# A hybrid DeltaNet and neighbourhood-attention layer on one core: PSUM pools that wait by bank, one more empty step before a group of transposes, and another order of the first loads

## The chip, the cores and the metric

The kernel runs on one core of one Trainium2 chip. The core has a matmul engine (TensorE, PE in the rows), a vector engine (VectorE, DVE), a scalar engine (ScalarE, ACT), a general one (GpSimd, POOL), and a synchronisation engine (SyncE, SP) that here only issues DMAs. Each engine runs its own instructions in order, and waits on semaphores for the others. SBUF is the on-chip memory that all of them read. PSUM is the memory that matmuls write, in eight banks of 128 x 512 fp32.

The metric is the device time of one execution in microseconds (us), the median of several runs.

## The reference

One layer, on 1024 latent tokens and 256 context tokens, of width 1024:

```python
mod_x = silu(c) @ w_ada + b_ada                    # shift, scale, gate, twice; the same for the context
px = modulate(rms_norm(x, norm1_w), sh1, sc1) @ w_in
pc = modulate(rms_norm(ctx, norm1_w), csh1, csc1) @ w_in
dn_c, s_f, s_b = gated_deltanet(pc[..., :DN_IN], ..., zeros, zeros)   # 4 heads of 128, chunks of 64
dn_x, _, _ = gated_deltanet(px[..., :DN_IN], ..., s_f, s_b)           # both directions
na_x = neighborhood_attention(qx, kx, vx, kc, vc, na_rpb, rows)       # 8 heads of 64, 8 x 16 window
x = x + g1 * (concat([dn_x, na_x]) @ w_out)
x = x + g2 * swiglu(modulate(rms_norm(x, norm2_w), sh2, sc2), w_ffn_in, w_ffn_out)
```

The DeltaNet group needs, for each chunk, the inverse of a unit lower triangular matrix I + M, where M is made of the keys' products kk, the decays g and the betas.

## The kernel before

Matrix products are done on fp32 values that are split into a rounded part and a remainder: three matmuls for each product, hi x hi, hi x lo and lo x hi. Normed and modulated tokens lie in `hh` and `hl` (eight tiles of 128 features x 1280 tokens, 256 of them context), weights in `whi` and `wlo`. `whi` is made by a cast (L201 or, on ScalarE, L203) of a raw tile `wraw` (or `fraw`, for the first two blocks), and `wlo` by a subtraction (L204, on POOL but for the first block, where DVE does it).

The first part of the program, up to the attention, is a list of jobs. A job is one column block of the input projection: eight k-steps of nine matmuls L413 into three banks `blk` (256, 512 and 512 tokens), or a `Wide` job, with tokens on the partitions, by L609. The order is k0, k1 (these two together, in the opening part, L757 and L413), k2, k3, z (second half), nk0, nk1, nk2, nv, nk3, q0 to q3, nq0 to nq3, v0, nv, v1 to v3, z (first half). Between the k-steps the code of the loop advances other work one step at a time, by Python generators: the `finish` of an earlier block (transposes L537, the products kk L561 and their copies L562), its `norm` (L502 to L516), and a background list `bg` that holds `block_inverses` and then `preps`. A `yield` without work in such a generator is an empty step: the work after it is issued one k-step later, and so stands further down in the order of every engine that takes part.

`block_inverses` begins with `decay_tables` (small DVE operations that give G, then L842 on TensorE), builds the matrices in `WK` (L865, L878, L880), transposes them on TensorE in four groups of eight (L900, `m<-cst,WK`), each group in two banks that ScalarE copies to `N` (L902). Then it inverts by back substitution on DVE (L910 and L912, for c from 30 down to 1, one c each k-step), and transposes back (L922).

In the opening part ScalarE squares the token tiles `xt`, TensorE sums them (L742), and the first modulation follows: `ada(j)` multiplies the 1 MB weight tile `wada` j with silu(c) (L706), the result is copied to `arow` (L708), `column(j)` brings it to the partitions (L714, L716, L719), and `normed_tile(k)` makes hh and hl (L726 and L729 on DVE, L727 on ScalarE). SP issues the loads on one queue, in the order of the code.

PSUM is handed out by pools, one after another. The opening part and k2, k3, z use `psb`, the jobs from nk0 on `psa` (four `blk` banks, two `m`, two `pr`), the last job and the attention `psg` (two tiles `sc` of three banks, two banks `ps`), and the output projection and the rest `psf` (eight banks). A new pool opens where an old one is closed. With no option given, every tile of the new pool waits for every user of the released ones.

## Time and profile before

| | us |
|---|---|
| median of 3 runs | 1517.0 (1516.87 to 1519.63) |
| the profiled execution | 1512.36 |
| its span | 1510.6 |
| TensorE busy in it | 1462.2 (97%) |
| VectorE, ScalarE, GpSimd busy | 996.8, 703.5, 236.7 |
| granted TensorE clock, mean | 0.996 of full |

Rows of the profile begin with the start (us from the span's start), the time that the merged group took, engine, line and operation; `out<-in` are the program's tile names; in brackets at the end stands the idle time of the engine just before, and what ended it. Rows of waits name the waiting and the releasing instruction, then the total in us, the count and the longest. A line number is that of the kernel before; in the changed kernel lines stand 7 to 13 further down.

### The profile page before, as it was taken

How to read it: one execution, taken by the hardware profiler on the slowest of the kernel's cores; microseconds unless marked ns; L12 is line 12 of the kernel's file. 1: busy time of each engine (PE TensorE's matmuls, PEld its weight loads, DVE VectorE, ACT ScalarE, POOL GpSimd, SP SyncE). 2: the span in 40 equal slices, each digit the busy share in tenths (PEclk: the TensorE clock that was granted, in tenths of full speed). 3: DMA queues.
4: the chain of work that ended last, by engine and by line, in shares of the span. 5: the costliest groups of instructions: out<-in, count | busy, mean ns of one | idle time of the engine just before them, and what ended most of it. 6: DMA issues, size and time to landing. Idle time of an engine off the chain costs nothing.

```text
span 1510.6 us, 23890 instructions
## 1 busy us (share of the span) xinstructions
PE 1462.2 (97%) x8702; PEld 1223.5 (81%) x8702; DVE 996.8 (66%) x1716; ACT 703.5 (47%) x1389; POOL 236.7 (16%) x286
## 2 busy tenths in 40 slices
PE   6999999999999998999999999999999999999998
PEld 3788797877788877887878888888888888888887
DVE  5773589875463745778867389766665567598652
ACT  5453442456663246656853284333333334354440
POOL 1054601456652201111210000000000000000000
PEclk9999999999999999999999999999999999999999
DMA  9274122778665569998539205433333335798742
GB/s 389 75 215 143 54 78 72 244 222 248 195 191 174 157 187 291 290 263 279 163 112 343 79 28 166 141 105 105 105 105 105 105 105 174 260 360 279 251 140 84
DMA packets 205398, 267.36 MB, mean 177 GB/s; under 512 B 15968, under 2 KB 113760, under 8 KB 204256
## 3 DMA queue, kind: packets, MB, share of 16 engines
q1 hardware_dynamic: 197680, 260.01, 53.2%
q10 hardware_dynamic: 7600, 5.81, 1.2%
q8 instruction: 69, 1.13, 0.3%
q14 instruction: 49, 0.40, 0.1%
HBM read 201.02 MB, written 68.94 MB: 179 GB/s over the span
## 4 chain that ended last, share of the span: by engine, by line
PE 51%; ACT 1%; DVE 1%; issue 0%; DMA 0%; POOL 0%; DVEq 0%; POOLq 0%; ACTq 0%
PE ps L1398 28%; PE ps L1741 14%; PE ps L1527 3%; PE ps L1375 1%; PE ps L1549 1%; PE sc L332 1%; PE sc L322 1%; PE sc L309 1%; PE ps L1252 0%; PE ps L1261 0%; DMA z<-z_d 0%; ACT sq L1302 0%; ACT bt L315 0%; DVE bt L313 0%; PE ps L223 0%
## 5 line engine op out<-in xcount | busy, mean ns | idle before, releaser
L1459 ACT CAST uhi<-wq 128x512 fp32r<-128x512 f32 x101 | 61.3, 622 | 135.9 <-issue 84.6
L413 PE MATMUL blk<-hh,whi 128*128 128x512 f32 (+1 forms) x410 | 121.0, 389 | 1.6 <-ACT kk L562 1.4
L1459 ACT CAST uhi<-ws 128x512 fp32r<-128x512 f32 x91 | 54.0, 621 | 146.3 <-PE ps L1398 91.4
L413 PE MATMUL blk<-hl,whi 128*128 128x512 f32 (+1 forms) x410 | 113.4, 370 | 0.3 <-DVE hl L729 0.3
L609 PE MATMUL blk<-zw,hh 128*128 128x256 f32 (+1 forms) x576 | 112.3, 289 | 1.0 <-ACT cr L461 1.0
L413 PE MATMUL blk<-hh,wlo 128*128 128x512 f32 (+1 forms) x410 | 112.0, 370 | 0.6 <-POOL wlo L204 0.6
L1460 DVE TENSOR_TENSOR ulo<-wq,uhi 128x512 fp32r<-128x512 f32 x101 | 67.6, 688 | 59.1 <-ACT uhi L1459 32.7
L1398 PE MATMUL ps<-hT,uhi 128*128 128x512 f32 x336 | 103.7, 390 | 0.0
L1398 PE MATMUL ps<-lT,uhi 128*128 128x512 f32 x336 | 103.4, 389 | 0.0
L1398 PE MATMUL ps<-hT,ulo 128*128 128x512 f32 x336 | 103.4, 389 | 0.0
L609 PEld LDWEIGHTS blk<-zw,hh 128*128 128x128 f32 x576 | 90.7, 189 | 4.1 <-ACT cr L461 1.4
L1398 PE MATMUL ps<-hB,uhi 128*128 128x512 f32 x288 | 89.1, 390 | 0.0
L1398 PE MATMUL ps<-lB,uhi 128*128 128x512 f32 x288 | 88.7, 389 | 0.0
L1398 PE MATMUL ps<-hB,ulo 128*128 128x512 f32 x288 | 88.7, 389 | 0.0
L413 PEld LDWEIGHTS blk<-hh,wlo 128*128 128x128 f32 x410 | 71.0, 188 | 14.8 <-POOL wlo L204 0.9
L413 PEld LDWEIGHTS blk<-hl,whi 128*128 128x128 f32 x410 | 71.2, 188 | 14.4 <-DVE hl L729 0.8
L609 PE MATMUL blk<-zw,hl 128*128 128x256 f32 (+1 forms) x288 | 81.9, 284 | 0.0
L413 PEld LDWEIGHTS blk<-hh,whi 128*128 128x128 f32 x410 | 67.6, 190 | 16.8 <-issue 3.8
L204 POOL TENSOR_TENSOR wlo<-wraw,whi 128x1024 fp32r<-128x1024 f32 x18 | 44.8, 2488 | 186.8 <-ACT whi L203 186.5
L1398 PEld LDWEIGHTS ps<-lT,uhi 128*128 128x128 f32 x336 | 63.1, 188 | 13.1
L1398 PEld LDWEIGHTS ps<-hT,ulo 128*128 128x128 f32 x336 | 63.1, 188 | 13.1
L1398 PEld LDWEIGHTS ps<-hT,uhi 128*128 128x128 f32 x336 | 62.9, 188 | 13.0
(361 smaller groups left out, 3500.7 us busy)
## 6 DMA issues: line engine op xcount, KB each, us to landing
wq<-w_fo SPq DMA_DIRECT2D x99, 256.0 KB, 4.2
wq<-w_gu SPq DMA_DIRECT2D x88, 256.0 KB, 2.9
wad<-wa SPq DMA_DIRECT2D x64, 256.0 KB, 4.3
bt<-rpb SPq DMA_DIRECT2D x64, 192.0 KB, 3.9
t_d<-g SPq DMA_DIRECT2D x22, 512.0 KB, 3.5
fr<-t_d SPq DMA_DIRECT2D x44, 256.0 KB, 4.9
f_d<-g SPq DMA_DIRECT2D x33, 256.0 KB, 2.1
fr<-f_d SPq DMA_DIRECT2D x33, 256.0 KB, 4.2
```

Of the source, the lines that this page charges most:

```text
L204: lo_engine.tensor_tensor(o, r, h.bitcast(F32), OP.subtract)
L309: s = pe.matmul(sc[:, u * 640 + n0:u * 640 + n1], q, ks[i], start=i == 0, stop=i == 1)
L322: pe.transpose(sc[:, u * 640 + j * 128:u * 640 + (j + 1) * 128], bt[:, j * 128:(j + 1) * 128], ident)
L332: pe.matmul(sc[u * ND:u * ND + ND, 1280:1408], vv, pt[:, j * 128:(j + 1) * 128], start=j == 0, stop=j == 4)
L413: pe.matmul(o, ww[:, k], xx[k][:, s], start=k == 0 and j == 0, stop=k == KT - 1 and j == 2)
L609: pe.matmul(p[:, :c1 - c0], x[k][:, s], ww[:, k, c0:c1], start=k == 0 and j == 0, stop=k == KT - 1 and j == 2)
L1375: pe.matmul(o, w[wi][:, k], parts[xi][k][:, s], start=k == 4 and j == 0, stop=k == 3 and j == 2)
L1398: pe.matmul(o, w[wi][:, k], x[xi][:, k], start=first and k == 0 and j == 0, stop=k == n - 1 and j == 2, skip_group_check=True)
L1459: act.copy(hi, self.raw[key])
L1460: dve.tensor_tensor(lo, self.raw[key], hi.bitcast(F32), OP.subtract)
L1527: pe.matmul(o, w[wi][:, k], parts[xi][k][:, s], start=k == 0 and j == 0, stop=k == KT - 1 and j == 2)
L1741: pe.matmul(o[b], w[wi][:, b], F[xn, p][xi], start=n in (0, 1, 5) and p == 0 and j == 0, stop=p == NFB // 2 - 1 and j == 2, skip_group_che ...
```

## The change

Three things are changed.

1. The pools `psa`, `psg` and `psf` are opened so that a tile waits only for the users of earlier tiles in its own bank. For the last job the two `sc` tiles get a pool of their own, `psc`, which is opened ahead of `psg` and of which the first tile is taken at once, so that `sc` lies in the first six banks and `ps` in the last two.
2. In `block_inverses` there are five empty steps and not four ahead of the first transposes L900, and none behind the last step of the back substitution: the transposes stand one k-step later, the rest of the work where it was.
3. `wada` 0 is loaded ahead of the two `fraw`; `ada(0)` is written ahead of the two weight splits; and the subtraction that makes the first block's `wlo` (DVE) is put off, into `normed_tile(0)`, between its three L726 and its three L729.

```diff
@@ -62,6 +62,13 @@
     live = [g for g in gens if g is not None]
     while live:
         live = [g for g in live if next(g, 0) != 0]
+
+
+class Deferred:
+
+
+    def tensor_tensor(self, *args):
+        self.args = args
 
 
 class Background:
@@ -292,7 +299,7 @@
         def pair(heads, bts, vw, vc, half, cb, out):
 
             r0 = 4 * half
-            sc = psum[-1].tile([128, 1536], F32, name="sc", tag="sc", bufs=2)
+            sc = psc.pop() if len(psc) > 1 else psc[0].tile([128, 1536], F32, name="sc", tag="sc", bufs=2)
             mx = nw.tile([128, 2, 4], F32, name="mx", tag="mx", bufs=3)
             for u, (head, w0, bt) in enumerate(zip(heads, WIN, bts)):
                 qs, kh, kl = head
@@ -368,7 +375,7 @@
         next(old)
         store(*done)
 
-    na, kept = [], []
+    na, kept, psc = [], [], []
 
     def store(out, hp, half):
 
@@ -680,9 +687,10 @@
                 sp.dma_start(x, a["xcT"][k])
                 xt.append(x)
             raws = [xp.tile([128, KT, 128], F32, name=f"fraw{i}", tag=f"fraw{i}") for i in range(2)]
+            load_ada(0)
             for i in range(2):
                 sp.dma_start(raws[i], a["w_conv"][4 + i])
-            for j in range(3):
+            for j in range(1, 3):
                 load_ada(j)
             sp.dma_start(cst, a["cst"])
             sp.dma_start(masks, a["masks"])
@@ -718,13 +726,15 @@
                                       [128, 2, 2]), OP.add)
                 dve.tensor_scalar(w1s[:, j], m[:, 1], 1.0, n1w[:, j:j + 1], op0=OP.add, op1=OP.mult)
 
-            def normed_tile(k, cuts=(slice(0, CT), slice(CT, T))):
+            def normed_tile(k, cuts=(slice(0, CT), slice(CT, T)), between=None):
                 t = xt[k]
                 parts = [(x, mod1[:, k, int(x.start < CT):int(x.start < CT) + 1]) for x in cuts]
                 for x, sh in parts:
                     j = int(x.start < CT)
                     dve.scalar_tensor_tensor(t[:, x], t[:, x], w1s[:, k, j:j + 1], rs[:, x], op0=OP.mult, op1=OP.mult)
                     act.activation(hh[k][:, x], t[:, x], AF.Identity, bias=sh)
+                if between:
+                    dve.tensor_tensor(*between.args)
                 for x, sh in parts:
                     dve.scalar_tensor_tensor(hl[k][:, x], t[:, x], sh, hh[k][:, x].bitcast(F32),
                                              op0=OP.add, op1=OP.subtract)
@@ -743,11 +753,12 @@
                 for p, s in zip(sums, segs):
                     act.activation(rs[:, s], p[:, :s.stop - s.start], AF.Ln, bias=b_eps, scale=1.0 / D)
                 act.activation(rs, rs, AF.Exp, scale=-0.5)
-                first[0].prefetch(raws[0], dve, dve)
+                ada(0, dve.tensor_copy)
+                kept_lo = Deferred()
+                first[0].prefetch(raws[0], kept_lo, dve)
                 first[1].prefetch(raws[1], pool, pool)
-                ada(0, dve.tensor_copy)
                 column(0)
-                normed_tile(0, segs)
+                normed_tile(0, segs, kept_lo)
                 ada(1, act.copy)
                 for b in first:
                     b.banks()
@@ -890,10 +901,8 @@
                         if not d:
                             yield
                     dve.transpose(fl(KKc), fl(Wc[1]))
-                    yield
-                    yield
-                    yield
-                    yield
+                    for _ in range(5):
+                        yield
                     for i0 in range(0, 32, 4):
                         p = bank()
                         for i in range(4):
@@ -910,7 +919,8 @@
                     dve.tensor_tensor(t, N[:P, :, 0:c, c:c + 1].to_broadcast([P, 4, c, w]),
                                       N[:P, :, c:c + 1, c + 1:32].to_broadcast([P, 4, c, w]), OP.mult)
                     dve.tensor_tensor(N[:P, :, 0:c, c + 1:32], N[:P, :, 0:c, c + 1:32], t, OP.add)
-                    yield
+                    if c != 30:
+                        yield
                 flat = N.rearrange("p b r c -> p b (r c)")
                 dve.memset(flat[:P, :, 0:1024:33], 1.0)
                 for _ in range(7):
@@ -1090,7 +1100,7 @@
             j = jobs[n] if n < len(jobs) else None
             if n == inv:
                 early.close()
-                psum.append(psa.enter_context(tc.tile_pool(name="psa", bufs=1, space=PSUM)))
+                psum.append(psa.enter_context(tc.tile_pool(name="psa", bufs=1, space=PSUM, reuse_waits="tile")))
                 bg.add(block_inverses())
                 bg.add(preps())
             final = n == len(jobs) - 1
@@ -1102,7 +1112,9 @@
                 next(fill)
             if final:
                 psa.close()
-                psum.append(scan_psum.enter_context(tc.tile_pool(name="psg", bufs=1, space=PSUM)))
+                psc.append(scan_psum.enter_context(tc.tile_pool(name="psc", bufs=1, space=PSUM, reuse_waits="tile")))
+                psc.append(psc[0].tile([128, 1536], F32, name="sc", tag="sc", bufs=2))
+                psum.append(scan_psum.enter_context(tc.tile_pool(name="psg", bufs=1, space=PSUM, reuse_waits="tile")))
             if n + 1 < len(jobs):
                 jobs[n + 1].prefetch()
             fin = blk(n - 2) if n - 2 not in done else None
@@ -1357,7 +1369,7 @@
         store(out, 3, half)
     attn.close()
     load_w = weights(wp)
-    ps = ctx.enter_context(tc.tile_pool(name="psf", bufs=8, space=PSUM))
+    ps = ctx.enter_context(tc.tile_pool(name="psf", bufs=8, space=PSUM, reuse_waits="tile"))
 
     def bank(name="ps"):
         return ps.tile([128, 512], F32, name=name, tag="ps")
```

Three places show what moves. The loads on SP at the start, before:

```order
L680 DMA xt_156<-xcT 128x1280
L680 DMA xt_158<-xcT 128x1280
L684 DMA fraw_160<-w_conv 128x1024
L684 DMA fraw_161<-w_conv 128x1024
L676 DMA wada<-wa 128x2048 x3
```

and after:

```order
L687 DMA xt_156<-xcT 128x1280
L687 DMA xt_158<-xcT 128x1280
L683 DMA wada<-wa 128x2048
L692 DMA fraw_160<-w_conv 128x1024
L692 DMA fraw_161<-w_conv 128x1024
L683 DMA wada<-wa 128x2048 x2
```

The first of the eight `wada` has passed both `fraw`. DVE there, before:

```order
L740 TENSOR_TENSOR sq_220<-sq_219,sq_220 128x512 x2
L201 CAST whi<-fraw_160 128x1024
L204 TENSOR_TENSOR wlo<-fraw_160,whi 128x1024
L708 COPY arow<-pm 128x256
L716 TENSOR_TENSOR mod_99<-pm,prm 128x2x2
L719 TENSOR_SCALAR w1s<-mod_99,prm 128x2
L726 SCALAR_TENSOR_TENSOR xt_144<-xt_144,w1s,rs 128x256
L726 SCALAR_TENSOR_TENSOR xt_144<-xt_144,w1s,rs 128x512 x2
L729 SCALAR_TENSOR_TENSOR hl_130<-xt_144,mod_99,hh_129 128x256
```

and after:

```order
L750 TENSOR_TENSOR sq_220<-sq_219,sq_220 128x512 x2
L716 COPY arow<-pm 128x256
L208 CAST whi<-fraw_160 128x1024
L724 TENSOR_TENSOR mod_99<-pm,prm 128x2x2
L727 TENSOR_SCALAR w1s<-mod_99,prm 128x2
L734 SCALAR_TENSOR_TENSOR xt_144<-xt_144,w1s,rs 128x256
L734 SCALAR_TENSOR_TENSOR xt_144<-xt_144,w1s,rs 128x512 x2
L737 TENSOR_TENSOR wlo<-fraw_160,whi 128x1024
L739 SCALAR_TENSOR_TENSOR hl_130<-xt_144,mod_99,hh_129 128x256
```

The copy of `arow` now stands ahead of the cast, and the subtraction behind the three products with `xt`. POOL's order does not change: it splits the second `fraw`, and then the weights of the later blocks.

The third place is job nk2. ScalarE there, before (N<-m are the copies L902, hl the norm's cast L515 of an earlier block, whi the cast of the next weights, cacc<-blk the emptying of nk2's own banks L446):

```order
L503 ACTIVATE cr<-m,bias 128x512
L503 ACTIVATE cr<-pr,bias 128x512
L203 CAST whi<-wraw 128x1024
L507 ACTIVATE cr<-cr 128x1280
L515 CAST hl_1623<-cacc 128x1280
L902 COPY N<-m 80x128x4 x8
L203 CAST whi<-wraw 128x1024
L446 ACTIVATE cacc<-blk 128x256
L446 ACTIVATE cacc<-blk 128x512 x2
```

and after:

```order
L514 ACTIVATE cr<-cr 128x1280
L522 CAST hl_1623<-cacc 128x1280
L911 COPY N<-m 80x128x4 x6
L210 CAST whi<-wraw 128x1024
L453 ACTIVATE cacc<-blk 128x256
L911 COPY N<-m 80x128x4 x2
L453 ACTIVATE cacc<-blk 128x512 x2
```

The last two copies to N now stand behind the cast and behind the first emptying. On TensorE the end of that job reads, before (L900 are the transposes, hh_458 belongs to the last k-step):

```order
L413 MATMUL blk<-hh_456,wlo 128x256
L413 MATMUL blk<-hh_456,wlo 128x512 x2
L900 MATMUL m<-cst,WK 80x128 x8
L413 MATMUL blk<-hh_458,whi 128x256
L413 MATMUL blk<-hh_458,whi 128x512 x2
L413 MATMUL blk<-hl_459,whi 128x256
L413 MATMUL blk<-hl_459,whi 128x512 x2
L413 MATMUL blk<-hh_458,wlo 128x256
L413 MATMUL blk<-hh_458,wlo 128x512 x2
L502 MATMUL m<-cr,cst 128x256
L502 MATMUL m<-cr,cst 128x512
L502 MATMUL pr<-cr,cst 128x512
```

and after:

```order
L420 MATMUL blk<-hh_458,wlo 128x256
L420 MATMUL blk<-hh_458,wlo 128x512 x2
L909 MATMUL m<-cst,WK 80x128 x8
L509 MATMUL pr<-cr,cst 128x512
L509 MATMUL m<-cr,cst 128x256
L509 MATMUL m<-cr,cst 128x512
```

Each group has moved down by one k-step, the last one to right ahead of the norm's matmuls.

## The prediction

> **What bounds the kernel now.** I read the page first (span, busy times, the chain that ended last), then the list of what TensorE waited for, then the clock by windows, and last the order of time around each place that the edits touch.
>
> The page of the kernel before:
>
> ```profile
> span 1510.6 us, 23890 instructions
> ...
> PE 1462.2 (97%) x8702; PEld 1223.5 (81%) x8702; DVE 996.8 (66%) x1716; ACT 703.5 (47%) x1389; POOL 236.7 (16%) x286
> ...
> PE ps L1398 28%; PE ps L1741 14%; PE ps L1527 3%; PE ps L1375 1%; PE ps L1549 1%; PE sc L332 1%; PE sc L322 1%; PE sc L309 1%; PE ps L1252 0%; PE ps L1261 0%; DMA z<-z_d 0%; ACT sq L1302 0%; ACT bt L315 0%; DVE bt L313 0%; PE ps L223 0%
> ```
>
> TensorE is busy for 1462.2 of 1510.6 us, so only 48.4 us can be won without removing matmuls, and the change removes none. The last row is the chain that ended last: nearly half of the span, the stretch from L1375 to the end, hangs on TensorE's own matmuls alone. All of the change's effect must come out of TensorE's idle time before that. It is this, by what ended it:
>
> ```profile
> PE m L742 <- DVE sq L740: 10.6, 1, 10.6
> ...
> PE m L900 <- ACT N L902: 1.4, 1, 1.4
> PE blk L413 <- ACT kk L562: 1.4, 1, 1.4
> PE m L922 <- DVE N L915: 1.3, 1, 1.3
> ...
> PE blk L609 <- ACT cr L461: 1.0, 1, 1.0
> PE pm L706 <- DMA wada<-wa: 1.0, 2, 0.8
> ...
> PE ps L1375 <- ACT no L334: 0.4, 1, 0.4
> ```
>
> The largest piece (10.6, the first loads) is not touched: the eight xT tiles stay in front of everything. The change points at five waits: L706 on `wada` (0.8 of the 1.0), L413 on `kk` (1.4, pool `psa`), L900 on `N` (1.4), L609 on `cr` (1.0, pool `psg`) and L1375 on `no` (0.4, pool `psf`). Together they are 5.0 us, 0.33% of the time. The reader's question at each is the same: if this wait goes, what does TensorE meet next, and was that late anyway?
>
> The clock matters too. By windows of 3.41 us (the halvings that the trace shows begin and end on multiples of this length):
>
> ```profile
> 20.69:24.10 3.41, 2.04 (x21) 1.02 (x20) 1.35 (x3) 2.19 (x3) 3.11 (x1) 1.00 1.00 416
> 24.10:27.51 3.41, 3.29 (x19) 1.47 (x20) 3.28 (x8) 2.15 (x4) 0.00 (x0) 0.50 1.03 417
> 27.51:30.93 3.42, 3.42 (x12) 2.94 (x12) 1.72 (x5) 0.20 (x1) 0.00 (x0) 0.50 1.02 422
> 290.34:293.75 3.41, 1.40 (x10) 0.98 (x9) 2.46 (x4) 3.21 (x5) 2.50 (x3) 1.00 0.99 319
> 95.78:99.19 3.41, 1.74 (x9) 1.12 (x9) 3.41 (x7) 1.70 (x3) 3.10 (x8) 1.00 0.70 221
> ```
>
> The columns after the length are busy us of PE, PEld, DVE, ACT, POOL, then the granted clock, the DMA share and GB/s. After the window with 2.04 us of PE work the clock was 0.50 for two windows; after 1.40 it was halved too (the window from 293.75), after 1.74 it was not. A halved window full of matmuls does half its work: 1.7 us lost each. So a wait that grows to about half of a window may cost 1.7 us on top.
>
> [...]
>
> **Part 1, the first modulation weights ahead of the blocks' weights, and wlo of the first block later.**
>
> ```profile
> 19.24 1.26 POOL L201 CAST whi<-fraw 128x1024 fp32r<-128x1024 f32 x1 [13.63 <-DMA fraw<-w_conv]
> ...
> 19.64 1.94 DVE L204 TENSOR_TENSOR wlo<-fraw,whi 128x1024 fp32r<-128x1024 f32 x1
> ...
> 20.58 3.23 POOL L204 TENSOR_TENSOR wlo<-fraw,whi 128x1024 fp32r<-128x1024 f32 x1
> ...
> 21.81 1.07 PE L706 MATMUL pm<-wada,wide 128*32 128x256 f32 x16 [0.76 <-DMA wada<-wa]
> ...
> 24.22 1.94 PE L706 MATMUL pm<-wada,wide 128*32 128x256 f32 x16 [0.19 <-DMA wada<-wa]
> ...
> 24.59 1.81 DVE L726 SCALAR_TENSOR_TENSOR xt<-xt,w1s,rs 128x256 f32<-128x256 f32 x3
> ...
> 25.77 1.38 ACT L727 ACTIVATE hh<-xt,mod 128x512 fp32r<-128x512 f32 x2 [0.15 <-DVE xt L726]
> ...
> 26.09 2.98 PE L757 MATMUL blk<-hh,whi 128*128 128x256 f32 x6
> ```
>
> One queue brings these loads in order, and 1 MB takes about 2.5 us (the second `fraw` is there at 19.24, the 1 MB `wada` behind it at 21.8, the next at 24.2; 1.05 MB at the 416 GB/s above is 2.5). In the new order `wada` 0 lands at about 19.3 and the two `fraw` at 20.5 and 21.8. TensorE starts ada(0) right behind its sums, 0.76 earlier. But TensorE's order still has ada(1) ahead of the first L757, and its weights have the same bytes in front of them: they land at 24.2 as before. So the 0.76 only moves to the wait at 24.22, and L757 cannot come before 26.09 at this clock. The gain is 0 here.
>
> What gets later is POOL: its L201 waits for the second `fraw`, 21.8 in place of 19.24, and L204 of the second block then runs from about 23.0. Alone it takes some 2.2 to 2.4 us (of its 3.23 the first 1.0 lay beside DVE's own L204, to 21.58; another L204, in part 3, takes 2.37), to about 25.3. DVE's L726 would be ready at about 23.8. It reads two SBUF tiles, and such an instruction stands still while POOL runs L204: a row of part 3 (197.80) has 2.71 us beside L204, where the first of its kind (196.10) takes 0.37. So L726 starts at 25.3 and not 24.59, 0.7 later; hh passes it on through ACT, and the first L757 come some 0.6 late. DVE's whi cast, now behind `arow`, lies beside the column's matmuls and ahead of 25.3: hidden. DVE's own wlo, now behind L726, takes at most 1.94 and is wanted by TensorE only behind these six matmuls (2.98) and the second column: covered. Term 1: **+0.6**. Lower end −0.9 (the clock is not halved in this stretch, so that ada(1) takes 1.07 in place of 1.94, and no collision); upper end +1.7 (one more halved window, because the later L757 leave the one from 27.51 emptier).
>
> **Part 2, psa waits by bank.**
>
> ```profile
> 140.68 2.94 POOL L566 TENSOR_TENSOR kd<-kk,cst 128x1280 f32<-128x1280 f32 x1 [9.71 <-ACT kk L562]
> ...
> 149.80 0.31 DVE L821 TENSOR_TENSOR G<-gA,nA 128x40 f32<-128x40 f32 x2
> ...
> 150.05 0.42 PE L842 MATMUL m<-G,cst 128*128 128x40 f32 x2 [0.41 <-DVE G L821]
> ```
>
> The first matmuls of nk0 no longer wait for `kk`, and TensorE runs 1.39 earlier for one k-step group. Then comes L842, which needs G. G comes from a run of small DVE operations, continuous since `kd`, which hangs on the same `kk` copy; nothing in that chain moves. L842 stays at 150.05, and its wait grows from 0.41 to 1.80. Term 2: **0**. The lower end is 0 (no instruction of the chain is earlier); the upper end +1.7, if 1.80 idle in the window 146.98 to 150.39 (1.6 busy) halves the next one.
>
> **Part 3, one more empty step ahead of the transposes L900.**
>
> ```profile
> 187.19 1.26 ACT L515 CAST hl<-cacc 128x1280 f16<-128x1280 f32 x1 [2.69 <-DVE cacc L510]
> ...
> 188.99 1.15 PE L900 MATMUL m<-cst,WK 128*80 128x128 f32 x8 [1.44 <-ACT N L902]
> ...
> 195.00 1.06 ACT L902 COPY N<-m 80x512 f32<-80x512 f32 x2 [1.57 <-PE m L900]
> 196.10 0.37 DVE L910 TENSOR_TENSOR tt<-N 80x120 f32<-80x120 f32 x1 [6.12 <-ACT N L902]
> ...
> 196.65 1.05 ACT L203 CAST whi<-wraw 128x1024 fp32r<-128x1024 f32 x1 [0.59 <-issue]
> ...
> 196.99 1.45 PE L502 MATMUL m<-cr,cst 128*128 128x256 f32 x4
> ...
> 197.61 1.35 ACT L446 ACTIVATE cacc<-blk 128x256 f32<-128x256 f32 x3
> 197.78 2.37 POOL L204 TENSOR_TENSOR wlo<-wraw,whi 128x1024 fp32r<-128x1024 f32 x1 [11.96 <-ACT whi L203]
> 197.80 2.71 DVE L910 TENSOR_TENSOR tt<-N 80x336 f32<-80x336 f32 x1
> ...
> 259.89 0.42 PE L922 MATMUL m<-cst,N 80*128 80x80 f32 x2 [1.29 <-DVE N L915]
> ```
>
> The wait of 1.44 goes: one k-step later ACT has passed L515 and emptied the banks. TensorE reaches the norm (L502) at 195.55 and not 196.99. But the last group of L900 now stands behind the last k-step, and ACT has the last two L902 behind L203 and the first L446. L203 came 0.34 ahead of L502; now a group of L900 (1.15) lies between them, so L203 starts at about 194.1. L203 1.05, L446's first part about 0.35 (of the 1.35 for its three) and two L902 1.06 end at 196.5, against 195.00 + 1.06 = 196.06: DVE's inverse (L910 and on) can start some 0.5 later. On the other side POOL's L204 follows L203 and runs from about 195.1 to 197.5, so that it blocks the inverse for 1.0 (196.5 to 197.5) and no longer for 2.3 (2.71 less some 0.4 for such an operation; the first took 0.37). The chain to L922 comes out 0.5 + 1.0 − 2.3 = −0.8. L922 waits for that chain already (1.29), so TensorE keeps what the chain gains, no more. Term 3: **−0.8**. Ends: −1.4 (all of the wait) and +0.5 (a later start and no relief from POOL).
>
> **Part 4, psc and psg.**
>
> ```profile
> 530.38 1.27 ACT L476 ACTIVATE cacc<-cacc 128x1280 f32<-128x1280 f32 x1 [0.54 <-DVE cacc L469]
> ...
> 532.11 0.60 PE L537 MATMUL m<-cst,cacc 128*128 128x128 f32 x4
> ```
>
> The 1.0 in front of L609 goes, since its bank was last used by an earlier copy. Some nine us on (532.11), TensorE's order has L537, which needs the SiLU L476 of the block before: this ends at 531.65 and hangs on DVE's convolution, which starts from the same `cr` as before. L537 can come 0.4 to 0.5 earlier, not 1.0. Term 4: **−0.5**, ends −1.0 and 0.
>
> **Part 5, psf.**
>
> ```profile
> 783.68 3.27 POOL L380 TENSOR_TENSOR na<-no,na 128x512 fp32r<-128x512 f32 x2 [19.56 <-ACT na L379]
> ...
> 786.34 1.17 PE L1375 MATMUL ps<-na,whi 128*128 128x512 f32 x4
> ```
>
> L1375 starts 0.4 earlier, runs dense, and meets the matmuls that read the last `na`. POOL finishes it at 783.68 + 3.27 = 786.95, in the middle of the row at 786.34; nothing of POOL's or ACT's work moves. Term 5: **−0.1**, ends −0.4 and 0. Behind it TensorE is dense to the end, so what is left here reaches the end.
>
> **The sum.** +0.6 + 0 − 0.8 − 0.5 − 0.1 = −0.8 us. The profiled execution took 1512.36 (span 1510.6), and would be at 1511.6. The runs' median is 1517.0, 4.6 above it, so the forecast for the median is 1517.0 − 0.8 = **1516.2**. A measurement of this kernel tells about 0.2% (3.0 us) from no change: this is "the same". The sum of the lower ends is −3.7 (1513.3), that of the upper ones +3.9 (1520.9); they will not all fall together.
>
> **Rivals.**
> A. All five waits go and nothing is late behind them: −5.0, **1512.0**. For it: each is a real idle of TensorE on a path that is 97% TensorE. Against it: the rows of L842, L922, L537 and L380, which come from chains that the change does not touch. It needs these to be shorter than they look.
> B. The clock: one of the two halved windows at the start goes, because ada(0) and the column lie differently in their window: 1.7 less, **1514.5**. For it: 2.04 us of work led to a halving and 1.74 elsewhere to none, so this window is near a border. Against: work only moves within it.
> C. Slower: at L842 the grown wait (1.80 idle, 1.6 busy) lies between the 1.40 that halved the clock and the 1.74 that did not. If it halves, and stays so for two windows as from 24.10, the price is 3.4: 1516.2 + 3.4 = **1519.6**. Slower than before it is from one window on (1516.2 + 1.7 = 1517.9); by over 0.2% only with two windows and 0.4 more.
>
> **Chances.** My sum 0.52 (by itself 1514.3 to 1518.0), A 0.20, B 0.15, C 0.13. Faster by over 0.2%: A, a quarter of B and a little of the sum, 0.27. Slower by over 0.2%: two fifths of C and a little of the sum, 0.10. The rest, 0.63, is the same. The range 1512.0 to 1519.3 leaves half of A below and most of C's two windows above.
>
> **What would show it.** In the profile after: L706's first idle gone and ada(1) still at about 24.2, with L726 not before 25 (step 1); L842 with about 1.8 of wait on G (step 2); no wait at L900, the first L910 at 196 to 197 and L922 still waiting for DVE (step 3); L609 without a wait and L537 with one of about 0.5 on `cacc` (step 4); L1375 on `na` from POOL, 0.4 (step 5). I am wrong if L842 or L922 start earlier by the whole of the wait removed, if the clock shows other halvings than two, or if L726 starts before 24.6.

## The result: 0.24% slower, and the profile after

The changed kernel takes 1518.2 us (median of 12 runs, 1514.7 to 1522.0) against 1516.1 for the kernel before (12 runs, 1511.0 to 1519.6). The ratio on record is 1.0024, with a 95% interval of 1.0013 to 1.0034; the two medians alone lie 2.1 us, 0.14%, apart. Forecast were 1516.2 and "the same", with a chance of 0.10 for slower by over 0.2%. The median lies inside the range given (1512.0 to 1519.3), but the direction is wrong: 0.8 us less were forecast, and the whole interval lies above 1.

The runs of one kernel spread by 7 to 9 us. Part of this is the clock: of the 12 runs of the changed kernel the three slowest (1520.9 to 1522.0) are those with the lowest mean clock, 0.989 and 0.990, and the six below 1518 have 0.993 to 0.995. The profiled execution took 1514.67 (span 1512.9, mean clock 0.993), 2.3 more than that of before (1512.36, clock 0.996).

Lines in the fences below are those of the kernel named. In the changed kernel L714 is ada, L727 w1s, L734 xt, L768 the first block matmuls, L853 the first decay matmul, L909 the transposes, L932 the transposes back. From the page of the changed kernel, and from the list of what TensorE waited for (total us, times, longest):

```profile
span 1512.9 us, 23888 instructions
...
PE 1466.1 (97%) x8702; PEld 1226.5 (81%) x8702; DVE 997.1 (66%) x1716; ACT 703.3 (46%) x1389; POOL 235.9 (16%) x286
```

```profile
PE m L932 <- DVE N L925: 2.2, 1, 2.2
PE m L853 <- DVE G L832: 2.1, 1, 2.1
...
PE pm L714 <- DMA wada<-wa: 1.1, 1, 1.1
...
PE blk L768 <- ACT hh L735: 0.9, 2, 0.6
...
PE blk L616 <- ACT zg L647: 0.5, 1, 0.5
...
PE ps L1387 <- POOL na L387: 0.3, 1, 0.3
```

The five waits that the change points at are gone from the list, as it meant. What the list has in their place are six others: 2.2 at the transposes back (1.3 before), 2.1 at the decay matmul (0.4 before), 1.1 at the weights of ada(1) (0.2 before), 0.9 at the first hh, 0.5 at an L609 (L616 here) that waits for ScalarE's copy zg, and 0.3 on the last na. (Some waits elsewhere moved too, by up to 1.7.) All in all TensorE's idle time fell, from 48.4 us to 46.8 (1512.9 − 1466.1). But TensorE is busy 3.9 us longer (1466.1 against 1462.2) with the same matmuls: it ran slower. The clock by windows says where (length, busy us of PE, PEld, DVE, ACT and POOL, granted clock, DMA share, GB/s):

```profile
24.35:34.59 10.24, 9.09 (x36) 6.22 (x37) 8.76 (x14) 3.81 (x6) 1.58 (x1) 0.50 1.02 420
```

```profile
150.65:154.06 3.41, 1.93 (x15) 1.89 (x16) 3.41 (x18) 0.36 (x3) 1.49 (x2) 1.00 0.57 176
154.06:157.47 3.41, 3.41 (x12) 2.72 (x11) 2.69 (x4) 0.13 (x2) 2.58 (x3) 0.50 0.00 0
259.87:263.29 3.42, 1.15 (x6) 0.55 (x4) 3.17 (x8) 1.64 (x2) 0.58 (x1) 1.00 0.34 90
263.29:266.70 3.41, 3.12 (x12) 2.64 (x13) 3.34 (x4) 0.85 (x2) 0.00 (x0) 0.50 0.93 259
```

Three halved windows at the start and not two, and one each behind the two waits that had grown, L853 and L932. With the one behind 297 us, which both kernels have, the half clock lasts 20.5 us in all, 10.2 before. In the changed kernel three dense L413 (256, 512 and 512 columns; L420 there) take 1.07 us at half clock (154.22 to 155.29) and 0.59 at full clock (159.08 to 159.67). So by estimate a halved window of dense matmuls costs 1.5 us (3.41 x 0.48 / 1.07; the prediction has half of 3.41, 1.7), and 10.3 us more of it are worth up to 4.6 us.

The same instruction in the two traces shows how the time came and went (starts in us, from the rows of both traces; where the rows merge several matmuls, it is the start of a single one inside):

| instruction of before | before | after | difference |
|---|---|---|---|
| first block matmul L757 | 26.09 | 27.13 | +1.0 |
| last of the first hl matmuls L757 | 32.14 | 34.59 | +2.4 |
| L413 that waited for kk | 140.60 | 141.00 | +0.4 |
| L842, decay | 150.05 | 152.13 | +2.1 |
| L413 some us later | 153.58 | 156.99 | +3.4 |
| L413 ahead of the first L900 | 173.36 | 177.03 | +3.7 |
| first L609 behind L900 and the norm | 198.74 | 200.71 | +2.0 |
| first L922 | 259.89 | 262.81 | +2.9 |
| L413 behind it | 262.59 | 266.65 | +4.1 |
| L609 that waited for cr | 523.47 | 526.17 | +2.7 |
| L1261 (waits for a DMA) | 567.60 | 569.59 | +2.0 |
| first L1375 | 778.05 | 779.88 | +1.8 |
| L1375 on the last na | 787.02 | 789.34 | +2.3 |

Behind the last row nothing changes to the end. Three of the waits that the change takes away are visible as a step down (−1.6 at L413 on kk, where it had been +2.0; −1.7 over the transposes L900; −1.1 at L609, where it had been +3.8), and each is followed by a step up.

### The profile page after: what moved, and what is told of

The parts are those of the page before. It is cut to its first block, busy times and chain, and to the rows that moved or that the text cites. A ratio compares the mean times of both kernels' runs of the same rounds, so it can differ in the third digit from the quotient of the medians.

```text
span 1512.9 us, 23888 instructions
## 1 busy us (share of the span) xinstructions
PE 1466.1 (97%) x8702; PEld 1226.5 (81%) x8702; DVE 997.1 (66%) x1716; ACT 703.3 (46%) x1389; POOL 235.9 (16%) x286
## 4 chain that ended last, share of the span: by engine, by line
PE 51%; ACT 1%; issue 1%; DVE 0%; POOLq 0%; POOL 0%; DVEq 0%; ACTq 0%
PE ps L1410 28%; PE ps L1753 14%; PE ps L1539 3%; PE ps L1561 1%; PE ps L1387 1%; PE sc L339 1%; PE sc L316 1%; PE sc L329 1%; PE ps L1285 0%; PE ps L1264 0%; PE ps L1273 0%; ACT sq L1314 0%; DVE bt L320 0%; PE ps L230 0%; ACT pt L332 0%
## 5 line engine op out<-in xcount | busy, mean ns | idle before, releaser
L420 PE MATMUL blk<-hh,whi 128*128 128x512 f32 (+1 forms) x410 | 122.0, 391 | 0.2
L420 PE MATMUL blk<-hl,whi 128*128 128x512 f32 (+1 forms) x410 | 114.5, 373 | 0.3 <-DVE hl L739 0.3
L420 PE MATMUL blk<-hh,wlo 128*128 128x512 f32 (+1 forms) x410 | 112.8, 372 | 0.6 <-POOL wlo L211 0.6
L616 PE MATMUL blk<-zw,hh 128*128 128x256 f32 (+1 forms) x576 | 112.2, 289 | 0.7 <-ACT zg L647 0.5
L616 PEld LDWEIGHTS blk<-zw,hh 128*128 128x128 f32 x576 | 90.7, 189 | 3.7 <-ACT zg L647 0.9
L420 PEld LDWEIGHTS blk<-hh,wlo 128*128 128x128 f32 x410 | 71.7, 190 | 15.0 <-POOL wlo L211 0.9
L420 PEld LDWEIGHTS blk<-hl,whi 128*128 128x128 f32 x410 | 72.0, 190 | 14.5 <-DVE hl L739 0.8
L616 PE MATMUL blk<-zw,hl 128*128 128x256 f32 (+1 forms) x288 | 81.8, 284 | 0.0
L420 PEld LDWEIGHTS blk<-hh,whi 128*128 128x128 f32 x410 | 68.3, 192 | 15.3 <-issue 3.8
L211 POOL TENSOR_TENSOR wlo<-wraw,whi 128x1024 fp32r<-128x1024 f32 x18 | 45.0, 2500 | 188.4 <-ACT whi L210 188.0
```

Of the source, the lines that this page charges most:

```text
L211: lo_engine.tensor_tensor(o, r, h.bitcast(F32), OP.subtract)
L420: pe.matmul(o, ww[:, k], xx[k][:, s], start=k == 0 and j == 0, stop=k == KT - 1 and j == 2)
L616: pe.matmul(p[:, :c1 - c0], x[k][:, s], ww[:, k, c0:c1], start=k == 0 and j == 0, stop=k == KT - 1 and j == 2)
```

## The experiments

The theory formed from this: the change takes out waits whose work is bound by the same late producers, so that TensorE's idle time is gathered at the next place; a gathered wait of 2 us empties a window of 3.41 us far enough that the next one runs at half clock; and at the start POOL's late subtraction blocks VectorE. The rival: the time was lost in the chains alone (DVE, POOL), and the clock only tells of it. All ratios are to the kernel before, on the same chip, in brackets the 95% interval.

### One part at a time

Each takes hunks of the diff above and leaves the rest as before: `s1_start` the third part, `s2_psa` this,

```diff
-psum.append(psa.enter_context(tc.tile_pool(name="psa", bufs=1, space=PSUM)))
+psum.append(psa.enter_context(tc.tile_pool(name="psa", bufs=1, space=PSUM, reuse_waits="tile")))
```

`s3_step` the hunks with `range(5)` and `c != 30`, `s4_scores` those of psc, psg and psf.

> Only the first part is changed: wada 0 loaded ahead of the two fraw, and the first block's wlo put off. Theory (collision and clock): POOL's L204 of the second block now runs from about 23.3 to 25.9 us and holds up DVE's w1s and xt (L727 and L734 of the changed kernel), so that the first block matmuls come 1.0 us later, and the half clock at the start lasts three windows of 3.41 us and not two; together 1.5 to 2.5 us slower than before. Rival (the prediction's own size): the collision alone, 0.6 us slower. Second rival (the start costs nothing, the loss is all behind it): within 0.3 us of before.

> Only the pool psa waits by bank. Theory (clock): TensorE passes the first matmuls of nk0 about 1.4 us earlier, waits about 1.8 us for G at L842, where the wait was 0.4, and in most executions the window behind it runs at half clock; 0.5 to 1.5 us slower than before, with a halved window at about 150 to 154 us in the profile. Rival (the prediction): the same wait of 1.8 us, no halving, 0.0 us. Second rival: G comes earlier too and TensorE gains 1 us or more.

> Only the empty step is moved. Theory (clock): the wait of 1.4 us at L900 goes, but the back substitution on DVE starts later or no earlier, and the wait at L922 grows from 1.3 to about 2 us; with a halved window behind L922 in part of the executions the change comes out between 0.8 us faster and 0.7 us slower. Rival (the prediction): 0.8 us faster, with no halved window there. Second rival: the whole 1.4 us is kept.

> Only the pools psc, psg and psf are changed. Both the theory and the prediction: the wait of 1.0 us at L609 goes, about half of it comes back at L537, and the 0.4 us at L1375 is given back where the last na is read; 0.4 to 1.0 us faster than before, and no new halved window, since no wait grows beyond 1 us. If it comes out slower, the loss of the whole change does not lie in the first 300 us alone.

| part | ratio | interval |
|---|---|---|
| s1_start | 1.0006 | 0.9997 to 1.0015 |
| s2_psa | 1.0005 | 0.9992 to 1.0017 |
| s3_step | 1.0009 | 0.9996 to 1.0022 |
| s4_scores | 1.0005 | 0.9991 to 1.0018 |

None differs from 1 by itself, and none is below 1. Together they are 0.25%, as the whole change, which may be chance: each interval is 0.18 to 0.27% wide. So the times alone tell no theory from the other; no part can be named as the one that loses. The 0.8 and 0.6 us faster that the prediction gave for s3 and s4 do not show. The profile of s1 shows the start as in the changed kernel: w1s stands for 2.12 us, the clock is half from 24.10 to 34.34 us, and ada(2) starts at 34.80, against 32.70 before. In the profile of s3 the clock is halved behind its L922 (261.7 to 265.1 us) and in four other stretches, 23.9 us in all. In that of s2 the windows lay otherwise, and the one with most of the wait at L842 was not followed by a halving,

```profile
144.83:148.25 3.42, 1.51 (x8) 0.94 (x6) 3.42 (x26) 0.00 (x0) 0.63 (x2) 1.00 0.41 127
148.25:151.66 3.41, 3.23 (x22) 2.97 (x23) 3.38 (x10) 0.49 (x3) 2.79 (x3) 1.00 0.21 64
```

with its L842 at 148.43, 1.6 before that of the kernel before, in an execution of which the start ran at full clock. So the clock is halved behind a wait of about 2 us at L842 in some executions and not in others (2.10 in the changed kernel, 2.09 in s2_psa). What decides between them is not shown.

### The loads at the start: w2_fraw1

The changed kernel, with the second `fraw` in front of `wada` 0:

```diff
+            sp.dma_start(raws[1], a["w_conv"][5])
             load_ada(0)
-            for i in range(2):
-                sp.dma_start(raws[i], a["w_conv"][4 + i])
+            sp.dma_start(raws[0], a["w_conv"][4])
```

> The changed kernel with the second fraw loaded ahead of wada 0 (and the first fraw behind it). Collision theory: POOL's cast and L204 of the second block are over by about 23 us, DVE's w1s takes 0.2 and not 2.1, xt (L726) starts at about 24.3 and not 26.05, the first block matmuls follow at about 26.1 and not 27.1; 0.8 to 2.0 us below the changed kernel. Rival (xt is late for another reason): L726 stays at about 26.

It measured 1.0003 (0.9988 to 1.0018). The rows at the start in order of time, of the changed kernel first:

```profile
22.14 1.04 POOL L208 CAST whi<-fraw 128x1024 fp32r<-128x1024 f32 x1 [16.63 <-DMA fraw<-w_conv]
...
23.26 2.67 POOL L211 TENSOR_TENSOR wlo<-fraw,whi 128x1024 fp32r<-128x1024 f32 x1
...
23.83 2.12 DVE L727 TENSOR_SCALAR w1s<-mod,prm 128x2 f32<-128x2 f32 x1
24.61 1.94 PE L714 MATMUL pm<-wada,wide 128*32 128x256 f32 x16 [1.14 <-DMA wada<-wa]
26.05 1.81 DVE L734 SCALAR_TENSOR_TENSOR xt<-xt,w1s,rs 128x256 f32<-128x256 f32 x3
...
27.13 0.58 PE L768 MATMUL blk<-hh,whi 128*128 128x256 f32 x1 [0.58 <-ACT hh L735]
```

and of w2_fraw1:

```profile
19.61 2.68 POOL L211 TENSOR_TENSOR wlo<-fraw,whi 128x1024 fp32r<-128x1024 f32 x1
...
22.67 0.68 DVE L208 CAST whi<-fraw 128x1024 fp32r<-128x1024 f32 x1
...
23.65 0.23 DVE L727 TENSOR_SCALAR w1s<-mod,prm 128x2 f32<-128x2 f32 x1
23.97 1.81 DVE L734 SCALAR_TENSOR_TENSOR xt<-xt,w1s,rs 128x256 f32<-128x256 f32 x3
24.45 1.07 PE L714 MATMUL pm<-wada,wide 128*32 128x256 f32 x16 [1.04 <-DMA wada<-wa]
...
25.45 0.98 PE L768 MATMUL blk<-hh,whi 128*128 128x256 f32 x2
```

In the changed kernel an operation on 128 x 2 numbers, w1s, stands for 2.12 us: from its start until 25.95, when POOL's L211 ends (23.26 + 2.67 = 25.93). With that subtraction over at 22.3 the same operation takes 0.23, xt starts 2.1 earlier and the first block matmul 1.7 (part of it by the clock, which was 1.00 from 20.1 to 30.3 us in the second execution). That the collision is the cause of the late xt is shown. Where the whole kernel's time is concerned, 1.0003 against 1.0024 is 3 us less, but the intervals overlap.

### Filling the waits, and an order that moved: w1_fill2, w3_all, w4_before

To take away the halvings without taking away the waits, matmuls with a result that is overwritten are put where TensorE would idle. w1_fill2 has eight ahead of L842 (this edit) and, likewise, eight ahead of L922:

```diff
+        def warm(p, n):
+            for _ in range(n):
+                pe.matmul(p[:, :512], hh[0][:, :128], hh[0][:, :512], start=True, stop=True)
...
             pg = bank()
+            warm(pg, 8)
```

w3_all has the same, eight ahead of the second L223 (a sum of the later modulation), four at the start (`warm0`, with the last squares `sq` and the ones matrix, ahead of the column, of ada(1) and of the first block matmul), and the loads of w2_fraw1. w4_before is the kernel before with one filling ahead of ada(0) and one ahead of the column, five at L922 and eight at L223.

> The changed kernel with eight idle-filling matmuls (128x512, their result overwritten) put right ahead of the first decay matmul (L842) and eight ahead of the first transpose back (L922), where it waits 2.1 and 2.2 us. They add 3.8 us of TensorE work. Clock theory: they lie inside the waits and keep the window busy, so no halved window follows either place, and the time is 1.0 to 2.5 us below that of the changed kernel (ratio to before about 1.0005 to 1.0015 where the changed kernel had 1.0024). Rival (the loss is in the chains of DVE and POOL): the time is that of the changed kernel or up to 0.5 us more.

> The changed kernel with the second fraw first, with the idle-filling matmuls at both waits, and with more of them at the start (four, 128x512, ahead of the column, of ada(1) and of the first block matmul) and ahead of the second sum of the later modulation (eight, L223). Clock and collision theory: halved windows are left only where nothing is filled (about 430, 548, 590), and the time is 4 to 6 us below the changed kernel, 2 to 3.5 us below before (ratio 0.998 to 0.999). Rival (chains): 1 to 1.5 us below the changed kernel from the loads alone, so about 1.0015.

> The kernel before with idle-filling matmuls alone: one ahead of ada(0) and one ahead of the first column, five ahead of L922 and eight ahead of the second L223. Clock theory: the halved windows behind 24 and 291 us are fewer, 1 to 3 us below before (ratio 0.998 to 0.9993). Rival (the clock is not what the time hangs on): 0 to 0.5 us above before.

They measured 1.0027 (1.0012 to 1.0041), 1.0011 (1.0002 to 1.0020) and 1.0045 (1.0031 to 1.0059). All are misses, and they tell nothing for or against the clock, since the order in which the build puts the instructions is not the same: by the traces 88 to 118 of the other matmuls stand in another place, and 33 to 53 instructions of DVE, ACT and POOL. New waits stand there, in w3_all for instance:

```profile
265.39 1.13 PE L952 MATMUL m<-cst,N 80*128 80x80 f32 x8 [1.77 <-ACT WK L956]
```

```profile
291.75 0.50 PE L1030 MATMUL pr<-rg,mr 128*128 128x512 f32 x1 [0.72 <-POOL rg L1018]
```

w3_all had a mean clock of 0.998 in its profiled execution, the best of all profiles here, and was still slower than before: a full clock does not help where the order makes new waits.

### Filling where nothing moves: x1_fillclean, z1_fillstart, y2_fill_g, and the changed kernel again

Fillings ahead of L842 and at the start move no other instruction: in the traces each engine has the order of the changed kernel, but for the fillings. x1_fillclean has eight ahead of L842 and four of 512 columns at the start, y2_fill_g only the eight, z1_fillstart only fillings at the start (256, 512 and 256 columns). y1_again is the changed kernel, unaltered.

> The changed kernel with idle-filling matmuls at two places whose addition moves no other instruction: four (128x512) at the start, one ahead of the column, two ahead of ada(1), one ahead of the first block matmul, and eight ahead of the decay matmul L842. Their results are overwritten. Clock theory: no halved window from 24 to 35 us and none from 150 to 158, and 1.5 to 3 us below the changed kernel (ratio to before 1.0005 to 1.0015). Rival (chains alone): as the changed kernel, 1.002 or more.

> The changed kernel itself, unaltered, on the same chip as the three below. Expected by both theories: 1.0015 to 1.003 of before, as at first.

> The changed kernel with the eight idle-filling matmuls ahead of L842 alone. Clock theory: the halving behind L842, seen in about half of the executions' phases, goes, 0.5 to 1.3 us below the changed kernel of this call; the three halved windows at the start stay. Rival (chains): within 0.3 us of it or above.

> The changed kernel with idle-filling matmuls at the start alone (256 columns ahead of the column, 512 ahead of ada(1), 256 ahead of the first block matmul); the loads and the collision stay as changed. Clock theory: xt still late (L726 at about 26), but no halved window, or one, from 24 to 35 us; 1 to 2 us below the changed kernel (1.0020 to 1.0024), so 1.0008 to 1.0015. Rival (the collision alone makes the loss at the start): as the changed kernel.

| kernel | ratio | interval |
|---|---|---|
| the changed kernel, first | 1.0024 | 1.0013 to 1.0034 |
| y1_again | 1.0020 | 1.0009 to 1.0032 |
| z1_fillstart | 1.0016 | 1.0004 to 1.0029 |
| y2_fill_g | 1.0009 | 0.9997 to 1.0022 |
| x1_fillclean | 0.9991 | 0.9983 to 1.0000 |

x1_fillclean does all that the changed kernel does and some 6 us of useless matmuls more, and is 0.3% faster than it, with intervals that are apart: more than the theory had forecast (1.0005 to 1.0015). Its profile has no halved window from 24 to 35 us (ada(1) takes 1.07 us, and 1.94 in the changed kernel) and none behind L842 (three L413 take 0.58 there, from 152.90 to 153.48). No chain of DVE, POOL or ACT is shortened by this. So the clock is a cause of the loss, and a large one: that is shown. How it divides between the two places is not: either filling alone lowers the ratio, but their intervals overlap with that of the changed kernel, and by the middle values the two together bring more than the sum of both.

The granted clock of all runs, and not of the profiled ones alone, says the same. Its mean is 0.9922 in the 12 runs of y1_again, 0.9952 in the 35 runs of before beside them, and 0.9968 in x1_fillclean (before beside it: 0.9952). A mean lower by 0.0030 is 9.1 us more at half clock in 1514 us; at 0.48 lost of 1.07, as in the rows of L413 above, that is worth 4.1 us, and the means of the times lie 2.8 us apart. By this estimate the clock took more than the whole loss, and the rest of the change gained up to 1.3 us.

All twenty traces can be counted too. Behind the first L842 the clock was halved in four of five traces with the wait of 2.1 us (not in s2_psa), in none of seven with the 0.4 of before, and in none of eight with fillings. Behind the first L922 it was halved in ten of eleven with a wait of 2.0 to 2.2 us (not in y2_fill_g), and in two of six with 1.3 (s1_start, y5_beststep). At the start, without fillings, the changed order has 3, 3, 2, 2 and 2 halved windows (the changed kernel, s1_start, y1_again, y2_fill_g, w1_fill2), and the order of before 2, 0, 2 and 2 (before, s2 to s4).

The window at L842 in y1_again, without filling, and in y2_fill_g, with it:

```profile
150.20:153.60 3.40, 1.79 (x14) 1.76 (x15) 3.40 (x19) 0.22 (x2) 1.35 (x2) 1.00 0.65 189
153.60:157.00 3.40, 3.40 (x11) 2.81 (x10) 2.82 (x4) 0.28 (x3) 2.71 (x3) 0.50 0.00 0
```

```profile
151.40:154.90 3.50, 3.25 (x22) 2.65 (x21) 3.50 (x16) 0.49 (x3) 1.83 (x2) 1.00 0.49 150
154.90:158.30 3.40, 3.40 (x19) 2.87 (x18) 2.35 (x4) 0.06 (x1) 2.48 (x4) 1.00 0.00 0
```

The fillings fit the wait: in y2_fill_g they run from 150.38, and the decay matmul waits another 0.24 for G, so they delay nothing.

```profile
150.38 2.01 PE L417 MATMUL m<-hh 128*128 128x512 f32 x8
152.63 0.41 PE L858 MATMUL m<-G,cst 128*128 128x40 f32 x2 [0.24 <-DVE G L836]
```

z1_fillstart shows the collision without the half clock. Its clock stays full from 24 to 35 us (ada(1) takes 1.07 us at 25.23, ada(2) 1.07 at 32.70), and POOL's L211 again holds up VectorE, this time in the cast:

```profile
22.95 2.35 POOL L211 TENSOR_TENSOR wlo<-fraw,whi 128x1024 fp32r<-128x1024 f32 x1
...
23.59 2.26 DVE L208 CAST whi<-fraw 128x1024 fp32r<-128x1024 f32 x1
...
26.28 1.81 DVE L740 SCALAR_TENSOR_TENSOR xt<-xt,w1s,rs 128x256 f32<-128x256 f32 x3
...
27.36 0.38 PE L775 MATMUL blk<-hh,whi 128*128 128x256 f32 x1 [0.43 <-ACT hh L741]
...
32.70 1.07 PE L719 MATMUL pm<-wada,wide 128*32 128x256 f32 x16
```

The first block matmul is as late as in the changed kernel. What each cause is worth there is read from the start of ada(2), behind the first block's matmuls; of before, of the changed kernel and of w2_fraw1 it is

```profile
32.70 1.07 PE L706 MATMUL pm<-wada,wide 128*32 128x256 f32 x16
```

```profile
35.16 1.07 PE L714 MATMUL pm<-wada,wide 128*32 128x256 f32 x16
```

```profile
30.40 1.07 PE L714 MATMUL pm<-wada,wide 128*32 128x256 f32 x16
```

With full clock it comes at 30.40 without the collision (w2_fraw1) and at 32.70 with it (z1_fillstart); with half clock at 32.70 without it (before) and at 35.16 with it (the changed kernel). So by these four executions the collision costs 2.3 to 2.5 us, and the half clock as much again; before paid only the second. This is an estimate: the four differ in other things too, z1_fillstart by its fillings and before by the order of its loads.

### The two undone: x4_fraw1nopsa, x3_beforefill

x4_fraw1nopsa is w2_fraw1 with the hunk of `psa` taken back; x3_beforefill is the kernel before with two fillings of 512 columns, ahead of ada(0) and of the column.

> Second fraw ahead of wada 0, and the pool psa waiting for all users as before (the scores' pools, psf and the empty step stay changed). Clock theory: without the long wait at L842 the halved window at 150 to 158 us goes, which costs 0.9 us on average: 0.5 to 1 us below the run with the loads alone (1.0003), about 0.9997. Rival (psa is worth its 1.4 us): 1 us above it.

> The kernel before with two idle-filling matmuls (128x512) at the start alone, one ahead of ada(0) and one ahead of the column; no other instruction moves. Clock theory: no or fewer halved windows at 24 to 31 us, the blocks' start 1 to 1.8 us earlier, kept to the end: ratio 0.999. Rival: 1.000 or a little above.

x4_fraw1nopsa measured 1.0008 (0.9995 to 1.0021) against 1.0003 with `psa` changed: the theory had said 0.5 to 1 us faster, and it is neither clearly faster nor clearly slower. What `psa` costs or brings on average stays open. x3_beforefill measured 1.0002 (0.9989 to 1.0015), a miss of 0.1%. Its profile shows one reason: a filling of 512 columns on `sq` and the ones matrix shows as two matmuls, about 1.0 us in all; ada(1) started at 25.19 (24.22 before), and one halved window (29.5 to 32.9) was left. Two such fillings in x1_fillclean:

```profile
24.08 1.96 PE L715 MATMUL pm<-sq,ones 128*128 128x512 f32 x4
```

### A version below both: x2_fraw1fill, y3_best, z2_best, y5_beststep

The changed kernel with the loads of w2_fraw1, eight fillings ahead of L842, and fillings at the start: two sorts, x2_fraw1fill with 512 columns ahead of the column and twice 512 ahead of ada(1), y3_best (and z2_best, the same kernel once more) with 256 and 512. y5_beststep is y3_best with the empty steps of the kernel before.

```diff
+            def warm0(p, n):
+                if n:
+                    pe.matmul(p[:, :n], M[C_ONE], sq[1][:, CT:CT + n], start=True, stop=True)
...
                 p, w = bank("pm"), aw.pop(j)
+                warm0(p, 512 if j == 1 else 0)
...
                 p, row = bank("pm"), rows.pop(j)
+                warm0(p, 256 if not j else 0)
```

> Second fraw ahead of wada 0 (no collision) and the idle-filling matmuls of the run before without the one ahead of the block matmuls. Clock and collision theory together: the first block matmuls at about 25.5 at full clock, all behind them 2 to 3 us ahead of before up to 260 us, and the end 1.5 to 3 us ahead of before (ratio 0.998 to 0.999). Rival (the fillings do nothing): as the run with the loads alone, 1.0003.

> Second fraw ahead of wada 0, eight idle-filling matmuls ahead of L842, and at the start one of 256 columns ahead of the column and one of 512 ahead of ada(1), which fit their waits of 0.55 and 1.04 us (a filling of 512 took about 1.0 us before). Theory: ada(1) at 24.4 and not 25.9, so 0.5 to 1.5 us below the run with larger fillings (0.9971): ratio 0.996 to 0.9975. Rival (size of the filling does not matter): 0.9971.

> The run with the second fraw first and the fitted fillings (0.9984) once more, to settle its size: 0.997 to 0.9985, below 1 with its whole interval.

> As the run above, but with the four empty steps of before. Clock theory: the wait of 1.4 us at L900 is back, the wait at L922 shorter than 2 us and less often followed by a halving; the two about cancel, within 0.8 us of the run above. Rival (the step is worth its 1.4 us): 1.4 us above it. Second rival (the step costs): 0.5 us or more below it.

x2_fraw1fill measured 0.9971 (0.9958 to 0.9984), y3_best 0.9984 (0.9971 to 0.9997), z2_best 0.9986 (0.9977 to 0.9996): 1511.1, 1511.6 and 1512.2 us, against 1514.4 to 1514.8 for the kernel before beside them. All three intervals lie below 1. That the fitted fillings are better than the larger ones, as expected, did not show. In z2_best's profile the start is this, at full clock:

```profile
23.81 0.23 DVE L737 TENSOR_SCALAR w1s<-mod,prm 128x2 f32<-128x2 f32 x1
24.14 1.81 DVE L744 SCALAR_TENSOR_TENSOR xt<-xt,w1s,rs 128x256 f32<-128x256 f32 x3
24.62 1.07 PE L723 MATMUL pm<-wada,wide 128*32 128x256 f32 x16
25.62 0.97 PE L779 MATMUL blk<-hh,whi 128*128 128x256 f32 x2
```

y5_beststep measured 0.9995 (0.9983 to 1.0006), 0.11% or 1.7 us above y3_best on the same chip. This speaks for the first rival, that the empty step is worth about its 1.4 us once nothing else is in the way; the intervals overlap, so it is not shown, and s3_step, at 1.0009, speaks the other way.

## Why the prediction was wrong

**The step that failed is the clock.** The working began with the sentence that all of the change's effect must come out of TensorE's idle time, and it added five terms at an unchanged clock; halved windows stood only in the upper ends of terms 1 and 2 and in rival C. Between the two profiles the idle time did fall, by 1.6 us, and the busy time grew by 3.9, because the half clock lasted 20.5 us and not 10.2. The prediction's own sign of being wrong, other halvings than two, was there: three halved windows at the start, and those behind L842 and L922. Term by term:

**Term 1 (+0.6) was mis-sized: it measured +1.0 at the first block matmul and +2.4 behind the hl matmuls.** The mechanism was the one written down: no gain from the earlier ada(0), ada(1) still at 24.2 to 24.6, POOL's subtraction in VectorE's way. Three sizes were off. The second fraw was used from 22.14, not 21.8. POOL's L211 ended at 25.93 and not at 25.3, for it started later and took 2.67 and not 2.2 to 2.4. And it caught w1s already, so that xt began at 26.05, not 25.3. Then came the third halved window, which the text had as the upper end (+1.7) and not in the sum. By the four executions compared above, the collision alone was worth 2.3 to 2.5 us at the start of ada(2), four times the term. Over the whole kernel the size is open: s1_start, the first part by itself, measured 1.0006, or 0.9 us, with an interval from −0.5 to 2.3.

**Term 2 (0) was right as a chain and wrong as a cost.** L842 waited 2.1 us for G and kept none of the gain. But the term took the clock as unchanged. Behind that wait it was halved in both profiles of the changed kernel, and TensorE stood at +3.4 after it and not +2.1: the upper end again.

**Term 3 (−0.8) was right up to L922.** From just ahead of L900 (+3.7 at 173 us) to L922 (+2.9) the change is −0.8, as the sum had it. The way there was as described: the last copies of N behind the cast and the first emptying, and a shorter collision with POOL.

```profile
198.70 0.38 ACT L453 ACTIVATE cacc<-blk 128x256 f32<-128x256 f32 x1
198.87 2.37 POOL L211 TENSOR_TENSOR wlo<-wraw,whi 128x1024 fp32r<-128x1024 f32 x1 [9.33 <-ACT whi L210]
...
200.06 1.32 DVE L919 TENSOR_TENSOR tt<-N 80x120 f32<-80x120 f32 x1 [6.37 <-ACT N L911]
...
262.81 0.42 PE L932 MATMUL m<-cst,N 80*128 80x80 f32 x2 [2.21 <-DVE N L925]
```

What it left out is that a wait moved from one place to another keeps its price only if the clock does not mind: in the kernel before, 1.4 at L900 and 1.3 at L922 made two waits that halved nothing, and in the changed one none and 2.2 made one that did. Over all traces it is two of six against ten of eleven. The window with the 2.2 (1.15 us of work) was followed by half clock, and +2.9 became +4.1.

**Term 4 (−0.5) was about right in size, and named the wrong wait.** It was −1.1 at L609 (from +3.8), of which 0.4 came back some nine us later, but not at L537:

```profile
534.22 1.27 ACT L483 ACTIVATE cacc<-cacc 128x1280 f32<-128x1280 f32 x1 [1.79 <-DVE cacc L476]
...
534.70 0.60 PE L544 MATMUL m<-cst,cacc 128*128 128x128 f32 x4
...
535.80 0.38 PE L616 MATMUL blk<-zw,hh 128*128 128x256 f32 x1 [0.51 <-ACT zg L647]
```

L537 (L544 here) started without a wait, before the SiLU that the term made it wait for had ended (534.22 + 1.27 = 535.49). The L609 behind it waited, for a copy to zg that ScalarE makes behind that SiLU. What was gained did not all reach the end: L1261 waits for a load of y that does not follow TensorE, and took part of the lateness away from both sides (its wait is 1.89 us in the kernel before and 0.79 in the changed one: +3.1 to +2.0).

**Term 5 (−0.1) was right:** the wait goes, and 0.3 of wait on POOL's last na comes in its place.

**The rivals.** A, that the waits go through to the end, is refuted at each of the five places by rows of the first profile after: ada(1) starts at 24.61, L842 and L922 wait 2.1 and 2.2 us for late producers, an L609 waits for zg and an L1375 for POOL's last na. B, a halving less at the start, went the other way. C was the mechanism, with the price and the place given (L842), but it was weighed as a single event with a chance of 0.13. It happened at three places of one execution. The clock stood in the working as an accident, though the edits at three places gather idle time and so all push in the same direction. A sum over places of (chance of a halving after minus before) times the estimated 1.5 us belonged into the sum itself. In the two profiles that is three halved windows more, up to +4.6 on a sum of −0.8; measured were +2.3 between these two executions and +2.1 between the medians. By the counts over all traces it is 0.8 of a window at L842, 0.6 at L922 and 0.9 at the start: 2.3 windows or 3.5 us, an estimate that would make of −0.8 about +2.7.

## What to carry to other kernels

On an engine that is 97% busy, ask of each wait that an edit removes where the idle time goes; if its producer does not get earlier, it joins the next wait, and one wait of 2 us can cost more than two of 1.3 and 1.4: here the clock was halved behind the first kind in ten of eleven traces and behind the second, at L922, in two of six. Idle time that can't be removed may be filled with matmuls on data that are there anyway, as long as the order of the rest does not move (0.9991 with such fillings, 1.0024 without); compare the orders of the two kernels before reading the time. When a load is moved past others, the work that it now delays on POOL may stand in VectorE's way even if nobody waits for its result: here an operation of 0.23 us stood for 2.12.

## What the runs showed of the hardware

The clock fell behind windows in which TensorE worked. Windows of 3.41 us with 1.15, 1.79 and 1.93 us of TensorE work by the profile (rows above, the last two with the small matmuls L853 in them) were followed by half clock; one with 1.51 in s2_psa was not, nor this one of the changed kernel:

```profile
587.55:590.97 3.42, 1.74 (x14) 1.28 (x12) 2.70 (x10) 1.14 (x3) 0.00 (x0) 1.00 0.96 303
```

In the profiles of before and of the changed kernel the two emptiest windows behind the first loads held 1.40 and 1.15 us of work, and half clock followed both. None there at full clock with more than 2.04 was followed by it, and in between both happened: it followed 1.51, 1.93, 1.99 and 2.04, and not 1.74, 1.95 and 2.00. Nor did one busy window always bring the clock back: in the changed kernel the halved window from 27.77 to 31.18 us held 3.17 us of work and was followed by another. The halvings behind the same wait come and go between executions (behind L842 at 154.1 us in one profile of the changed kernel, at 153.6 in the other, none in s2_psa).

VectorE's stop beside POOL took in small operations too: w1s, on 128 x 2 numbers, stood for 2.12 us beside an L211 of 2.67 in the changed kernel and took 0.23 without it in w2_fraw1, and a cast that took 0.68 in w2_fraw1 stood for 2.26 beside an L211 of 2.35 in z1_fillstart.
